# A two-layer encoder on one core: the row scale spread through memory, one multiply on VectorE, the last stores on one queue

## The chip, the core and the metric

The kernel runs on one core of a Trainium2 chip. Its engines work side by side, each through its own instructions in order, and wait for each other through semaphores: TensorE (PE in the profile; its weight loads are PEld), VectorE (DVE), ScalarE (ACT), GpSimd (POOL) and SyncE (SP), which here only issues DMAs. DMAs can be issued from SP, ACT or POOL; the transfers run on 16 DMA engines that all queues share. Matmul results land in PSUM, everything else on the chip lies in SBUF with 128 partitions, and "memory" means the DRAM beside the chip.

The metric is device time in microseconds of one execution. The kernel before was run three times.

## What is computed

A sequence of 256 tokens with 2048 features passes through two residual layers and a last RMS norm:

```
def rms_norm(x, g):
    xf = x.astype(jnp.float32)
    y = xf * lax.rsqrt(jnp.mean(xf * xf, axis=-1, keepdims=True) + EPS)
    return (y * g.astype(jnp.float32)).astype(x.dtype)

def reference(x, norm_g, final_g, w_in_even, w_out_even, rpb_b, w_in_odd, w_out_odd,
              sinks_c, qnorm_d, knorm_d):
    h = x
    for layer in range(DEPTH):
        y = rms_norm(h, norm_g[layer])
        i = layer // 2
        if layer % 2 == 0:
            h = h + even_layer(y, w_in_even[i], w_out_even[i], rpb_b[i])
        else:
            h = h + odd_layer(y, w_in_odd[i], w_out_odd[i], sinks_c[i], qnorm_d[i], knorm_d[i])
    return rms_norm(h, final_g)
```

Each layer multiplies the normed tokens by one wide input projection, runs two kinds of attention of 8 heads each on the results, gates them with a SiLU path, and multiplies by an output projection. All of it is float32.

## The kernel before

Every product is made from three matmuls: each float32 operand is split into a rounded high part and the remainder (`hi` and `lo`), and `mm3` (L100) adds hi·hi, hi·lo and lo·hi. Weights come from memory in blocks of 128 x 1024 (`Weights`, L54): SP loads the block into `wraw` (5 buffers), ScalarE writes `whi` (L69), VectorE writes `wlo` (L70), 3 buffers each. So each weight block costs one ScalarE and one VectorE instruction, and TensorE follows with the matmuls of that block. `by_feature` (L258) uses a block as the stationary operand (L267, L271), `by_token` (L277) as the moving one (L102 to L104).

The norm's gain per feature is multiplied into the tokens when they are split (`split`, L89, with `gcol`): ScalarE writes `xh` (L95) and VectorE `xl` (L96). The norm's scale per token, `r` or `rstd` (two columns of 128 tokens, L179), is not ready then; it is multiplied into the projections' results afterwards. Where tokens lie on partitions, a column of `r` does. Where tokens lie along the free axis (results of `by_feature`), every partition needs all 256 scales in a row. `spread_scale` (L187) makes that row: for each half a 128 x 128 tile `rb` whose row p holds the scale of token p (VectorE, from `ones`), a transpose of it on TensorE (L193) into the PSUM tile `ps_bc`, and a copy to `rk` (L196). From `rk` come `rq` (L197) and `rhalf` (L199), used in `scaled` (L307) for the queries, keys and gates. It runs once per layer: in `first_scale` (L585, near 43 us) and `second_scale` (L669, near 485 us).

The opening: 15 matmuls on zeros (`WARM`, L124) keep TensorE busy until the first operands arrive. The first product runs `by_token` over 8 blocks; with each block come two 128 x 256 blocks of x (`xraw`), split on the way (L71 to L74), and behind them the same x in the other layout (`load_h`, L136), whose squares give the first `r`.

The end: the last output product is made for token half 0, then for half 1 in two column halves. For each, `added` (L777) adds it to the residual and sums squares, `scale_of` (L788) makes the scale, and `finish` (L798) multiplies the four column blocks of 512 and stores each. Blocks 1 and 2 of half 1 are multiplied on ScalarE and stored from ACT's queue, the others are multiplied on VectorE and stored from SP's; blocks 0 and 3 are done in halves of 256 columns.

The order of instructions on each engine is fixed before the run by a planner that keeps the priority of program order but lets an instruction pass another that, by the planner's estimate of times, is not ready yet. What is wrapped in `pin`, `pinned` or `tc.keep_in_program_order` keeps its written order on its engine: nearly all DMAs on SP and the whole end.

Of the kernel before, what the change touches and what calls it, by code (L numbers as in the profile page):

```python
# [9 lines left out]
F32 = mybir.dt.float32  # L10
# [8 lines left out]
P = 128  # L19
D = 2048  # L20
S = 256
# [6 lines left out]
SCALE = HD ** -0.5  # L28
BIG = 1e30
GRID_W = 64  # L30
WARM = 15
AHEAD = 2
RPB_R, RPB_C = 15, 31

# [2 lines left out]
def encoder(ctx, tc, a, out):  # L37
    nc = tc.nc
    pool = lambda name, bufs, **kw: ctx.enter_context(tc.tile_pool(name=name, bufs=bufs, **kw))
    const = pool("const", 1)  # L40
# [4 lines left out]
    tp = pool("tp", 2)  # L45
    sm = pool("sm", 4)
    PS = bass.MemoryType.PSUM
    dram = pool("dram", 1, space=bass.MemoryType.DRAM)
    ps_mm = pool("ps_mm", 2, space=PS)
    ps_at = pool("ps_at", 3, space=PS)  # L50
# [3 lines left out]
    class Weights:  # L54


        def __init__(self, src, hi=None, lo=None, x=None):
            raw = wp.tile([P, 1024], F32, tag="wraw", name="wraw")
            self.hi = hi or hp.tile([P, 1024], F32R, tag="whi", name="whi")
            self.lo = lo or hp.tile([P, 1024], F32R, tag="wlo", name="wlo")  # L60
            cuts = KK if x in (0, 1) else 1
            cols = [slice(i * 1024 // cuts, (i + 1) * 1024 // cuts) for i in range(cuts)]
            for i, c in enumerate(cols):
                load = nc.sync.dma_start if x is None else pinned
                load(raw[:, c], src[:, c])
                if x is not None and i == 0:
                    pinned(xraw[x], a["xt"][x].rearrange("p (k t) -> p k t", k=KK))
            for i, c in enumerate(cols):
                nc.scalar.copy(self.hi[:, c], raw[:, c])  # L69
                nc.vector.tensor_sub(self.lo[:, c], raw[:, c], self.hi[:, c].bitcast(F32))  # L70
                if x is not None:  # L71
                    for m in (i,) if cuts > 1 else range(KK):
                        k = x * KK + m
                        split(xh[k], xl[k], xraw[x][:, m, :], gcol[:, k : k + 1])  # L74

    plan, ready = [], []

# [7 lines left out]
    def pinned(dst, src, **kw):  # L85

        tc.keep_in_program_order(nc.sync.dma_start(dst, src, **kw))

    def split(hi, lo, src, scale=None):  # L89

        if scale is None:
            nc.scalar.copy(hi, src)
            nc.vector.tensor_sub(lo, src, hi.bitcast(F32))
        else:
            nc.scalar.mul(hi, src, scale)  # L95
            nc.vector.scalar_tensor_tensor(  # L96
                out=lo, in0=src, scalar=scale, in1=hi.bitcast(F32), op0=ALU.mult, op1=ALU.subtract
            )
# [10 lines left out]
    xh = [X[k // 4][:, k % 4, 0, :] for k in range(KC)]  # L109
    xl = [X[k // 4][:, k % 4, 1, :] for k in range(KC)]  # L110
# [3 lines left out]
    xraw = [big.tile([P, KK, S], F32, tag=f"mh{j}", name="xraw") for j in range(NJ)]  # L114

    gcol = const.tile([P, 2 * KC], F32, tag="gcol", name="gcol")
# [6 lines left out]
    ps_idle = ps_o.tile([P, S], F32, tag="o", name="ps_idle")  # L123
    for _ in range(WARM):  # L124
        nc.tensor.matmul(ps_idle, idle[:, :P], idle, start=True, stop=True, skip_group_check=True)

    ident = const.tile([P, P], F32, tag="ident", name="ident")
    ones = const.tile([P, P], F32, tag="ones", name="ones")
    cosT = const.tile([P, 2, P], F32, tag="cosT", name="cosT")
    sinT = const.tile([P, 2, P], F32, tag="sinT", name="sinT")  # L130
    maskB = const.tile([P, S], F32, tag="maskB", name="maskB")
# [4 lines left out]
    def load_h(n):  # L136
        x = a["x"].rearrange("(t p) d -> p t d", p=P)
        pinned(h[n], x[:, :, n * 512 : (n + 1) * 512])
# [32 lines left out]
    def square_sums(parts, n, t=None):  # L171

        for tt in range(2) if t is None else (t,):
            junk = tp.tile([P, 512], BF16, tag="junk", name="junk", bufs=1)
            tc.keep_in_program_order(
                nc.scalar.activation(junk, h[n][:, tt, :], AF.Square, accum_out=parts[:, tt, n : n + 1])
            )
# [8 lines left out]

    def spread_scale(r):  # L187

        bc = ps_at.tile([P, S], F32, tag="at", name="ps_bc")
        for tt in range(2):  # L190
            t = tp.tile([P, P], F32, tag="rb", name="rb")
            nc.vector.tensor_scalar_mul(t, ones, r[:, tt : tt + 1])
            nc.tensor.transpose(bc[:, tt * P : (tt + 1) * P], t, ident)  # L193
        rk = const.tile([P, S], F32, tag="rk", name="rk")
        rq = const.tile([P, S], F32, tag="rq", name="rq")
        nc.vector.tensor_copy(rk, bc)  # L196
        nc.vector.tensor_scalar_mul(rq, rk, -SCALE)  # L197
        rhalf = const.tile([P, S], F32, tag="rhalf", name="rhalf")
        nc.vector.tensor_scalar_mul(rhalf, rk, 0.5)  # L199
        return rk, rq, rhalf  # L200
# [114 lines left out]
    def scaled_split(tag, acc, rbc):  # L315
        dst = pair(tag)
        split(*dst, scaled(acc, rbc))
        return dst

    def values(dst, acc, r):  # L320
        hi, lo = dst
        for t in range(2):
            split(hi[:, t, :], lo[:, t, :], acc[t], r[:, t : t + 1])
# [252 lines left out]
    def opening(j):  # L576
        if j == 2:
            make_identity(nc, ident)
            nc.gpsimd.memset(ones, 1.0)
        if j > 3:  # L580
            load_h(j - 4)
        if j == 7:
            square_sums(parts0, 0)

    def first_scale():  # L585
        for n in range(1, NN):
            square_sums(parts0, n)
            yield
        r = row_scale(0, parts0)
        yield  # L590
        yield
        scales[0] = r, spread_scale(r)
        yield
# [21 lines left out]
    for u in range(4):  # L615
        st = {}
        if u == 1:
            bg.append(later_consts())
        for pr, kind in even_order(u):
            if kind != "v":  # L620
                evac.append(evict_even(2 * u + pr, kind, by_feature(), st))
                continue
            if u:
                acc = by_token(512, token_acc())
            else:
                acc = [ps_at.tile([P, 512], F32, tag="at", name="ps_t") for _ in range(2)]
                by_token(512, acc, opening)
                evac.append(first_scale())
            st["v"] = values_tile()
            evac.append(evict_even(2 * u, kind, acc, st))  # L630
# [38 lines left out]
    def second_scale():  # L669
        for _ in range(4):  # L670
            yield
        scales[1] = spread_scale(r1)
        yield
# [88 lines left out]
    pin = tc.keep_in_program_order  # L762
    full, halves = slice(0, 512), [slice(0, 256), slice(256, 512)]
# [13 lines left out]
    def added(t, c, acc, others=None):  # L777
        ss = col("ss")
        add_y3(t, c, acc)
        junk = tp.tile([P, 512], BF16, tag="junk", name="junk", bufs=1)  # L780
        if others is None:
            pin(nc.scalar.activation(junk[:, c], y3(t, c), AF.Square, accum_out=ss))
        else:
            y = y3(t, c)
            pin(nc.vector.tensor_tensor_reduce(junk[:, c], y, y, 1.0, others, ALU.mult, ALU.add, ss))
        return ss

    def scale_of(ss, t):  # L788

        root, y, half, u, r = [col(name) for name in ("root", "y", "half", "u", "r")]  # L790
        pin(nc.scalar.activation(root, ss, AF.Sqrt, bias=sums[:, t : t + 1], scale=1.0 / D))
        pin(nc.vector.tensor_scalar(half, ss, -0.5 / D, minus[:, t : t + 1], ALU.mult, ALU.add))
        pin(nc.vector.reciprocal(y, root))
        pin(nc.vector.tensor_scalar(u, y, y, half, ALU.mult, ALU.mult))
        pin(nc.vector.tensor_scalar(r, u, 1.5, y, ALU.add, ALU.mult))
        return r

    def finish(n, t, r, cols=full, scalar=False):  # L798
        y = h[n][:, t, cols]
        if n == NN - 1:  # L800
            pin(nc.vector.scalar_tensor_tensor(y, y, r, gfin[n][:, cols], ALU.mult, ALU.mult))
        elif scalar:
            pin(nc.scalar.mul(y, y, r))  # L803
        else:
            pin(nc.vector.tensor_scalar_mul(y, y, r))
        queue = nc.scalar if scalar and t else nc.sync
        pin(queue.dma_start(out[t * P : (t + 1) * P, n * 512 + cols.start : n * 512 + cols.stop], y))

    for j, pr in enumerate(late):
        product_out(accs[0], final[j], pr, 0, False, j == 3)  # L810
    r = scale_of(added(0, full, accs[0]), 0)
    finish(0, 0, r)
    finish(2, 0, r, scalar=True)
    finish(1, 0, r)
    finish(3, 0, r)
    for j, pr in enumerate(late[:3]):
# [6 lines left out]
        ss = added(1, c, z[:, c], ss)  # L823
    r = scale_of(ss, 1)
    finish(0, 1, r, halves[0])
    finish(1, 1, r, scalar=True)
    finish(0, 1, r, halves[1])
    finish(2, 1, r, scalar=True)
    finish(3, 1, r, halves[0])
    finish(3, 1, r, halves[1])  # L830

# [82 lines left out]
```

## Time and profile before

| | us |
|---|---|
| three runs: median | 821.35 |
| lowest, highest | 820.9, 821.37 |
| profiled execution: time | 820.54 |
| its span, first to last instruction | 818.8 |
| TensorE clock granted, mean | 0.996 |

The span is the time that the profile shows; the 1.74 us between it and the execution's time lie outside the first and last instruction. Rows of the profile name an instruction by its line, engine and operation, then `out<-in`. In a timeline row the first number is the start in us from the span's start and the second the busy time; `x2` joins neighbours of one kind; the brackets give the engine's idle time before it and what ended that. ACTq, SPq and POOLq are the engines' own sequencers, which issue DMAs. A row `A <- B: 0.4, 1, 0.4` says that A waited for B for 0.4 us in total, once, at most 0.4.

### The profile page before, as it was taken

The numbers are of one execution on the slowest core, as the hardware profiler recorded it, in microseconds if no ns is written. First come the engines' busy times: TensorE is split into PE (matmuls) and PEld (weight loads), VectorE is DVE, ScalarE is ACT, GpSimd is POOL, SyncE is SP. The second block draws the span as 40 slices with busy tenths as digits, with TensorE's granted clock in tenths as the row PEclk, the third lists the DMA queues.
The fourth block names the chain that finished last, engine by engine and source line by source line (L and its number), as shares of the span: only waits on it lengthen the run. The fifth ranks groups of instructions, "written<-read, shape, count | busy, mean of one in ns | idle before, by whom it ended". The sixth has DMA issues, their size and how long they took to land.

```text
span 818.8 us, 11775 instructions
## 1 busy us (share of the span) xinstructions
PE 808.6 (99%) x4317; PEld 695.1 (85%) x4317; DVE 576.1 (70%) x856; ACT 447.3 (55%) x712; POOL 110.6 (14%) x88
## 2 busy tenths in 40 slices
PE   9999999999999999999999999999999999999995
PEld 7888888888888888888888888888899888888884
DVE  6677675677857886587655577685987777775763
ACT  7745454554545554455445544657666665664651
POOL 0002020021302140050200000002112222221000
PEclk9999999999999999999999999999999999999998
DMA  8956765575755766565654555556577775777532
GB/s 336 354 210 209 271 213 177 208 213 168 233 182 171 241 173 220 203 194 197 213 177 172 186 186 172 200 192 198 161 183 226 224 222 184 227 197 225 209 126 104
DMA packets 90682, 166.91 MB, mean 204 GB/s; under 512 B 48960, under 2 KB 50112, under 8 KB 90560
## 3 DMA queue, kind: packets, MB, share of 16 engines
q1 hardware_dynamic: 90192, 165.61, 62.5%
q8 instruction: 34, 0.56, 0.3%
q10 hardware_dynamic: 432, 0.54, 0.2%
q14 instruction: 24, 0.20, 0.1%
HBM read 155.64 MB, written 3.05 MB: 194 GB/s over the span
## 4 chain that ended last, share of the span: by engine, by line
PE 98%; DMA 0%; ACT 0%; DVE 0%; issue 0%; ACTq 0%; DVEq 0%
PE ps_f L267 34%; PE ps_f L271 17%; PE ps_t L102 14%; PE ps_t L103 14%; PE ps_t L104 14%; PE ps_s L103 1%; PE ps_s L104 1%; PE ps_s L102 1%; PE ps_out L103 1%; PE ps_out L102 1%; PE ps_out L104 1%; PE ps_ht L660 0%; DMA wraw<-in_even_t 0%; PE ps_tr L372 0%; ACT h L803 0%; ACT whi L69 0%
## 5 line engine op out<-in xcount | busy, mean ns | idle before, releaser
L70 DVE TENSOR_TENSOR wlo<-wraw,whi 128x1024 fp32r<-128x1024 f32 (+1 forms) x270 | 344.4, 1276 | 187.8 <-ACT whi L69 187.3
L69 ACT CAST whi<-wraw 128x1024 fp32r<-128x1024 f32 (+1 forms) x270 | 281.9, 1044 | 300.9 <-PE ps_t L104 130.7
L267 PE MATMUL ps_f<-x,whi 128*128 128x512 f32 x1184 | 372.3, 396 | 0.0
L271 PEld LDWEIGHTS ps_f<-x,wlo 128*128 128x128 f32 x1184 | 222.4, 188 | 52.9 <-DVE wlo L70 0.7
L271 PE MATMUL ps_f<-x,wlo 128*128 128x256 f32 x1184 | 233.0, 278 | 0.0
L267 PEld LDWEIGHTS ps_f<-x,whi 128*128 128x128 f32 x1184 | 180.9, 189 | 0.5
L102 PE MATMUL ps_t<-whi,x 128*128 128x512 f32 (+1 forms) x256 | 96.8, 381 | 0.3 <-ACT x L95 0.3
L103 PE MATMUL ps_t<-wlo,x 128*128 128x512 f32 (+1 forms) x256 | 96.4, 379 | 0.0
L104 PE MATMUL ps_t<-whi,x 128*128 128x512 f32 (+1 forms) x256 | 96.1, 377 | 0.0
L463 POOL COPY ph<-pr 128x1024 uint16<-128x1024 uint16 x32 | 39.5, 1233 | 418.1 <-ACT pr L453 252.0
L102 PE MATMUL ps_t<-whi,mh 128*128 128x512 f32 x240 | 93.8, 391 | 0.0
L103 PE MATMUL ps_t<-wlo,mh 128*128 128x512 f32 x240 | 93.7, 391 | 0.0
L104 PE MATMUL ps_t<-whi,ml 128*128 128x512 f32 x240 | 93.6, 390 | 0.0
L104 PEld LDWEIGHTS ps_t<-whi,x 128*128 128x128 f32 x256 | 48.5, 189 | 9.0
L102 PEld LDWEIGHTS ps_t<-whi,x 128*128 128x128 f32 x256 | 48.5, 189 | 9.0 <-ACT x L95 0.6
L474 POOL COPY pt<-pa 128x1024 uint16<-128x1024 uint16 x32 | 50.4, 1576 | 37.5 <-DMA pa<-ph 37.2
L103 PEld LDWEIGHTS ps_t<-wlo,x 128*128 128x128 f32 x256 | 48.6, 190 | 8.2
L104 PEld LDWEIGHTS ps_t<-whi,ml 128*128 128x128 f32 x240 | 45.1, 188 | 9.3
L103 PEld LDWEIGHTS ps_t<-wlo,mh 128*128 128x128 f32 x240 | 45.1, 188 | 8.9
L102 PEld LDWEIGHTS ps_t<-whi,mh 128*128 128x128 f32 x240 | 45.1, 188 | 8.9
L445 ACT ACTIVATE pr<-lg,mn 128x256 f32<-128x256 f32 (+1 forms) x48 | 24.0, 501 | 16.5 <-POOL ph L463 8.9
L403 POOL TENSOR_TENSOR bias<-maskB,rpb 128x512 f32<-128x512 f32 x8 | 12.5, 1567 | 138.5 <-DMA rpb<-rows 138.5
(129 smaller groups left out, 664.4 us busy)
## 6 DMA issues: line engine op xcount, KB each, us to landing
wraw<-in_even_f SPq DMA_DIRECT2D x96, 512.0 KB, 3.5
wraw<-in_odd_f SPq DMA_DIRECT2D x56, 512.0 KB, 3.7
wraw<-in_w_out_even SPq DMA_DIRECT2D x32, 512.0 KB, 3.3
wraw<-in_w_out_odd SPq DMA_DIRECT2D x32, 512.0 KB, 4.3
wraw<-in_even_t SPq DMA_DIRECT2D x30, 512.0 KB, 4.3
wraw<-in_odd_t SPq DMA_DIRECT2D x24, 512.0 KB, 3.2
xraw<-in_xt SPq DMA_DIRECT2D x8, 256.0 KB, 7.0
h<-in_x SPq DMA_DIRECT2D x4, 512.0 KB, 8.6
```

The source lines that it names most:

```text
L69: nc.scalar.copy(self.hi[:, c], raw[:, c])
L70: nc.vector.tensor_sub(self.lo[:, c], raw[:, c], self.hi[:, c].bitcast(F32))
L102: nc.tensor.matmul(dst, lh, rh, start=first, stop=False, skip_group_check=True)
L103: nc.tensor.matmul(dst, lh, rl, start=False, stop=False, skip_group_check=True)
L104: nc.tensor.matmul(dst, ll, rh, start=False, stop=last, skip_group_check=True)
L267: nc.tensor.matmul(acc[:, f, :], w.hi[:, c], xx[k], start=k == 0, stop=False, skip_group_check=True)
L271: nc.tensor.matmul(acc[:, f, :S], w.lo[:, c], xh[k], start=False, stop=k == KC - 1, skip_group_check=True)
L403: nc.gpsimd.tensor_tensor(b, maskB.unsqueeze(1).to_broadcast([P, 2, S]), raw, op=ALU.subtract)
L445: nc.scalar.activation(p[:, t, :W], lg[:, t, :W], AF.Exp, bias=mn[:, t : t + 1], scale=-1.0, accum_out=den[:, t : t + 1],)
L463: nc.gpsimd.tensor_copy(halves, words)
L474: nc.gpsimd.tensor_copy(words.bitcast(U16).rearrange("p c (q s) -> p s c q", s=2), st[i])
```

## The change

Three places. `spread_scale` no longer uses VectorE's `ones`, TensorE and PSUM: GpSimd's queue writes `r` to a line of 256 floats in memory, and then reads that line into all 128 partitions as `rk`. In the opening, the first block of x (k = 0) is multiplied on VectorE instead of ScalarE, and there are 14 matmuls on zeros instead of 15. At the end all five stores of token half 1 go through SP's queue, the two halves of block 0 follow each other, and block 3 is done whole.

```
-WARM = 15
+WARM = 14
...
-                        split(xh[k], xl[k], xraw[x][:, m, :], gcol[:, k : k + 1])
+                        split(xh[k], xl[k], xraw[x][:, m, :], gcol[:, k : k + 1], on=nc.vector if k == 0 else None)
...
-            nc.scalar.mul(hi, src, scale)
+            if on is None:
+                nc.scalar.mul(hi, src, scale)
+            else:
+                on.tensor_scalar_mul(hi, src, scale)
...
     def spread_scale(r):
 
-        bc = ps_at.tile([P, S], F32, tag="at", name="ps_bc")
-        for tt in range(2):
-            t = tp.tile([P, P], F32, tag="rb", name="rb")
-            nc.vector.tensor_scalar_mul(t, ones, r[:, tt : tt + 1])
-            nc.tensor.transpose(bc[:, tt * P : (tt + 1) * P], t, ident)
+        line = dram.tile([2, P], F32, tag="line", name="line")
+        nc.gpsimd.dma_start(line.rearrange("t p -> p t"), r)
         rk = const.tile([P, S], F32, tag="rk", name="rk")
+        nc.gpsimd.dma_start(rk, line.rearrange("t p -> (t p)").partition_broadcast(P))
         rq = const.tile([P, S], F32, tag="rq", name="rq")
-        nc.vector.tensor_copy(rk, bc)
         nc.vector.tensor_scalar_mul(rq, rk, -SCALE)
...
-        queue = nc.scalar if scalar and t else nc.sync
-        pin(queue.dma_start(out[t * P : (t + 1) * P, n * 512 + cols.start : n * 512 + cols.stop], y))
+        pin(nc.sync.dma_start(out[t * P : (t + 1) * P, n * 512 + cols.start : n * 512 + cols.stop], y))
...
     finish(0, 1, r, halves[0])
+    finish(0, 1, r, halves[1])
     finish(1, 1, r, scalar=True)
-    finish(0, 1, r, halves[1])
     finish(2, 1, r, scalar=True)
-    finish(3, 1, r, halves[0])
-    finish(3, 1, r, halves[1])
+    finish(3, 1, r)
```

The tile `ones` and its memset (L579) go as well.

More of the change, by code (lines that the diff above doesn't have):

```diff
@@ L87, in pinned, with split @@
         tc.keep_in_program_order(nc.sync.dma_start(dst, src, **kw))
-    def split(hi, lo, src, scale=None):
+    def split(hi, lo, src, scale=None, on=None):
         if scale is None:
@@ L127, in encoder @@
     ident = const.tile([P, P], F32, tag="ident", name="ident")
-    ones = const.tile([P, P], F32, tag="ones", name="ones")
     cosT = const.tile([P, 2, P], F32, tag="cosT", name="cosT")
@@ L578, in opening @@
             make_identity(nc, ident)
-            nc.gpsimd.memset(ones, 1.0)
         if j > 3:
```

## The prediction

> **What bounds the kernel now.** I read the page's busy times and its chain by engine first, then the busy time by stage (columns: stretch and length, then busy us and instructions of PE, PEld, DVE, ACT and POOL, the granted clock, DMA share, GB/s), then the waits of the first 30 us.
>
> ```profile
> PE 808.6 (99%) x4317; PEld 695.1 (85%) x4317; DVE 576.1 (70%) x856; ACT 447.3 (55%) x712; POOL 110.6 (14%) x88
> ...
> PE 98%; DMA 0%; ACT 0%; DVE 0%; issue 0%; ACTq 0%; DVEq 0%
> ```
>
> ```profile
> 60.00:480.00 420.00, 420.00 (x2272) 361.56 (x2271) 292.01 (x382) 215.32 (x311) 60.67 (x41) 1.00 0.62 202
> ...
> 500.00:800.00 300.00, 300.00 (x1617) 258.73 (x1616) 224.03 (x363) 179.22 (x318) 49.13 (x40) 1.00 0.63 195
> ```
>
> ```profile
> PEld ps_f L271 <- DVE wlo L70: 0.4, 1, 0.4
> ```
>
> TensorE is the path: 420.00 of 420.00 us and 300.00 of 300.00 us are busy at clock 1.00. In such a stretch a matmul less is time less, and work of another engine counts only when it makes TensorE wait. The last row is the exception: at 28.6 us TensorE once waits for a weight block. So the change is weighed in four places: the opening, the two spreads of the row scale (45 and 489 us), and the tail.
>
> **TensorE slots that go.** Four transposes (L193), two per layer.
>
> ```profile
> 42.92 0.63 PE L267 MATMUL ps_f<-x,whi 128*128 128x512 f32 x2
> ...
> 44.31 0.63 PE L267 MATMUL ps_f<-x,whi 128*128 128x512 f32 x2
> ...
> 45.02 0.38 PE L193 MATMUL ps_bc<-ident,rb 128*128 128x128 f32 x2
> ...
> 45.95 0.62 PE L267 MATMUL ps_f<-x,whi 128*128 128x512 f32 x2
> ```
>
> ```profile
> 488.50 0.39 PE L104 MATMUL ps_t<-whi,x 128*128 128x512 f32 x1
> ...
> 489.18 0.39 PE L104 MATMUL ps_t<-whi,x 128*128 128x512 f32 x1
> 489.41 0.38 PE L193 MATMUL ps_bc<-ident,rb 128*128 128x128 f32 x2
> ...
> 490.10 0.40 PE L104 MATMUL ps_t<-whi,x 128*128 128x512 f32 x1
> ```
>
> Durations overlap, so I take the distance of starts. In layer 0 two periods of the loop take 44.31 - 42.92 = 1.39 us, and 45.95 - 44.31 = 1.64 us with the transposes inside: 0.25 us. In layer 1 three matmuls take 489.18 - 488.50 = 0.68 us, and 490.10 - 489.18 = 0.92 us with them: 0.24 us. Nothing else fills these slots, so **-0.49 us**.
>
> **The scale through memory.** Two multiplies by `ones` and the copy out of PSUM leave VectorE. In their place POOL's queue, otherwise empty there, gets a store of 256 single floats and, behind its completion, a read of 1 KB into each of 128 partitions. No matmul reads `rk`; but VectorE runs in order, and `rq`, `rhalf` and the first product with `rq` stand among the weight blocks `wlo` that TensorE needs.
>
> ```profile
> 42.89 0.16 DVE L168 SCALAR_TENSOR_TENSOR rstd<-rs_t,rs_z 128x2 f32<-128x2 f32 x1
> ...
> 46.34 1.22 DVE L70 TENSOR_TENSOR wlo<-wraw,whi 128x1024 fp32r<-128x1024 f32 x1
> 47.47 0.29 DVE L197 TENSOR_SCALAR rq<-rk 128x256 f32<-128x256 f32 x1
> ...
> 47.88 0.69 DVE L312 TENSOR_TENSOR qf<-qf,rq 128x512 f32<-128x512 f32 x1
> 49.13 1.23 DVE L70 TENSOR_TENSOR wlo<-wraw,whi 128x1024 fp32r<-128x1024 f32 x1 [0.57 <-ACT whi L69]
> ...
> 490.70 1.22 DVE L70 TENSOR_TENSOR wlo<-wraw,whi 128x1024 fp32r<-128x1024 f32 x1
> ```
>
> ```profile
> 51.29 0.39 PE L271 MATMUL ps_f<-x,wlo 128*128 128x256 f32 x2
> ...
> 54.08 0.39 PE L271 MATMUL ps_f<-x,wlo 128*128 128x256 f32 x2
> ...
> 495.34 0.39 PE L103 MATMUL ps_t<-wlo,x 128*128 128x512 f32 x1
> ```
>
> ```profile
> rpb<-rows SPq DMA_DIRECT2D x32, 64.0 KB, 2.7
> ...
> sink<-in_sinks_c SPq DMA_DIRECT2D x1, 4.0 KB, 6.7
> ```
>
> ```profile
> DMA to landing us min/median/max: 1.9/2.6/3.3
> ```
>
> Counting weight blocks from the opening (2.79 us of TensorE each in layer 0, with three buffers of `wlo` running ahead), the `wlo` of 46.34 is first read at 51.29, that of 49.13 at 54.08, that of 490.70 at 495.34. The scale is ready at 43.05. If `rq` stays where it is, ahead of the block of 49.13, that block must start by 54.08 - 1.23 = 52.85, with 1.1 us (47.47 to 48.57) ahead of it: `rk` may land as late as 51.75, **8.7 us** after the scale. Should the order put `rq` one block earlier, the bound is 51.29 - 1.22 - 1.1 = 48.97, or **5.9 us**. Layer 1 has as much room: its block starts at 490.70 and is read 4.64 us later, against 4.95 us in both rows of layer 0.
>
> The trip itself is not in the trace. Stores land in 1.9 to 3.3 us (last row, those of `out`), reads in 2.7 (`rpb`, from the chip's memory) to 6.7 us (`sink`, in a burst). What POOL's queue takes to issue is not shown: between 0.33 us, an issue on SP (tail, below), and 1.04 us, the excess of a disturbed VectorE block over 1.23 us (below). I take 1.0 for each, since software on POOL is nearer to a POOL instruction: 2.0 + 2.6 + 2.7 = **7.3 us**, between 0.66 + 1.9 + 2.7 = 5.3 and 2.1 + 3.3 + 6.7 = 12.1. At 7.3 and the present order the cover holds: **0**, with 2 x 3.4 us at the far end. The attention that a later `rk` would delay starts only here:
>
> ```profile
> 65.68 0.42 DVE L429 CUSTOM_DVE_ANT_0 lg<-ps_s,bias 128x256 f32<-128x256 f32 x1
> ```
>
>
> The Trainium skill, page "DMA: Bandwidth & Descriptors", section "Anatomy of one DMA — SWDGE (gpsimd) path", fits about 2.0 us plus bytes over 436 GB/s per transfer; as an estimate that makes 2.0 + 2.3 = 4.3 us here, and the sum the same.
>
> **The opening.** One warm-up matmul goes, and the first multiply of `x` moves from ScalarE to VectorE.
>
> ```profile
> 4.50 0.69 DVE L70 TENSOR_TENSOR wlo<-wraw,whi 128x512 fp32r<-128x512 f32 x1 [3.35 <-ACT whi L69]
> 4.53 0.91 ACT L95 ACTIVATE x<-xraw,gcol 128x256 fp32r<-128x256 f32 x2
> 5.09 0.80 PE L102 MATMUL ps_t<-whi,x 128*128 128x512 f32 x1 [0.32 <-ACT x L95]
> ```
>
> ```profile
> 26.28 1.05 ACT L69 CAST whi<-wraw 128x1024 fp32r<-128x1024 f32 x1 [2.23 <-DMA wraw<-in_even_f]
> ```
>
> ```profile
> 27.36 1.23 DVE L70 TENSOR_TENSOR wlo<-wraw,whi 128x1024 fp32r<-128x1024 f32 x1 [2.08 <-ACT whi L69]
> ```
>
> ```profile
> 28.05 0.61 PE L267 MATMUL ps_f<-x,whi 128*128 128x512 f32 x2
> 28.64 0.50 PE L271 MATMUL ps_f<-x,wlo 128*128 128x256 f32 x2
> ```
>
> ```profile
> 2.00:26.00 24.00, 23.68 (x100) 19.68 (x100) 16.28 (x26) 15.88 (x28) 0.00 (x0) 1.00 1.00 377
> ```
>
> The nearest VectorE multiply of this size is 0.29 us (47.47), ScalarE's 0.91 / 2 = 0.45: the first matmul can start 0.2 us earlier, if the multiply goes ahead of `wlo`; behind it, 4.50 + 0.69 + 0.29 = 5.48, it starts 0.4 us later. Neither reaches the end in full. From 2 to 26 us the DMA engines are full (share 1.00, 377 GB/s); ScalarE gets the ninth block at 26.28 after 2.23 us of waiting for it, VectorE ends `wlo` at 28.59, and TensorE reads it at 28.64, some 0.12 us after it would have (28.05 + 0.47). A head start ends in that wait; a late one costs what exceeds 0.12. **0**, between -0.2 and +0.3. The warm-up matmul only frees an engine that then waits for `x`.
>
> **The tail.** Five stores on SP's queue instead of four there and two on ACT's, and ScalarE no longer issues between its two multiplies.
>
> ```profile
> 812.73 0.33 SPq L807 DMA_DIRECT2D out<-h  x1
> ```
>
> ```profile
> L807 SPq DMA_DIRECT2D out<-h x8: 332/382/448, 807.8 to 814.4; - x8
> ```
>
> ```profile
> 813.60:816.60 3.00, 0.00 (x0) 0.00 (x0) 0.15 (x1) 0.64 (x1) 0.00 (x0) 0.50 0.98 345
> ```
>
> The first half still leaves at 812.73, and from 813.6 to 816.6 the DMA engines are full (0.98): 1.05 MB at 345 GB/s is 3.0 us. Five issues 0.45 us apart reach 814.5, as late as now (814.4), with data always queued. Fewer small rows may help a little: **-0.1**, between -0.3 and +0.6 (a landing of 3.3 instead of 2.6 us).
>
> **Sum**: -0.49 + 0 + 0 - 0.1 = -0.6. The profiled execution would go from 820.54 to 819.9 (span 818.8 to 818.2). The median of the three runs, 821.35, stands 0.81 above that execution; from it the forecast is **820.8**.
>
> **Rivals.** *Slower: VectorE stands behind a late `rk`.* The point is 5.9 or 8.7 us for the trip. With 7.3 us and `rq` one block earlier TensorE loses 1.4 us per layer: 820.8 + 2.8 = **823.6**. For it speaks that the order is fixed before the run; against it, the present order and 2 us of margin at the short trip.
>
> *POOL and VectorE keep each other waiting.*
>
> ```profile
> 619.46 2.27 DVE L70 TENSOR_TENSOR wlo<-wraw,whi 128x1024 fp32r<-128x1024 f32 x1 [0.68 <-ACT whi L69]
> ```
>
> Here a `wlo` took 2.27 instead of 1.23 us while POOL copied. One such hold, 1.04 us, on each transfer makes the trip 9.4, 0.7 us over the bound per layer: 820.8 + 1.4 = **822.2**; with `rq` earlier as well, 3.5 per layer: 827.8. The Trainium skill, page "SBUF — State Buffer", section "SBUF: two separate sides", warns of it: transfers issued from GpSimd starve while VectorE runs a two-port operation, 3100 instead of 620 ns in its example. The trace agrees that the two engines hold each other; no run here yet shows it for a transfer.
>
> *The opening's head start survives*, because the loads come earlier than the trace suggests: 820.8 - 0.2 = **820.6**. *The parts don't do what they say*: the multiply sits behind `wlo` or the single queue ends late, +0.3 or +0.7, about **821.4**.
>
> **How the numbers follow.** A measurement of this kernel can tell about 0.2%, 1.6 us, from no change. Forecast 820.8 (820.2 to 821.3): 0.56. Head start: 0.06. Parts that don't act: 0.17. Late `rk`: 0.14. Mutual waiting: 0.07. The last two pass +1.6 us for most of their weight, 0.14. No case here passes -1.6 us; for what the trace does not show I leave 0.03. Within: 0.83. The range runs from all gains together, 820.8 - 0.2 - 0.2 - 0.4 of spread between runs = 820.0, to 823.0, inside the late `rk`.
>
> **What would show it.** Right: no L193; loop starts near 45 and 489 us at even distance; TensorE without a wait between 30 and 800; the wait for `wlo` near 28.6 still there, longer by the head start; stores full from 813 to 816. Wrong: a wait of TensorE for `wlo` just after 50 or 492 us, VectorE idle before L197 for over 4 us, or a stretch after the last store that is longer than now.

## The result, and the profile after

| | before | after |
|---|---|---|
| median, us | 820.97 (6 runs) | 838.81 (6 runs) |
| lowest to highest, us | 820.64 to 821.37 | 836.98 to 840.17 |
| ratio after / before | | 1.0215 (1.0201 to 1.0228) |
| profiled execution: time, us | 820.54 | 839.16 |
| its span, us | 818.8 | 837.3 |

The changed kernel is slower by 17.84 us. The forecast was 820.8 us, with a range up to 823.0. The line numbers below are those of each kernel's own file. In the changed kernel the store of the scale is L192, its read back L194, `rq` L196, `rhalf` L198, and `spread_scale`'s transposes are gone; `ps_f` is made at L266 and L270, `mm3` is L105 to L107.

First the page after: the busy times, then the chain that ended last, by engine and by line.

```profile
PE 814.2 (97%) x4312; PEld 698.3 (83%) x4312; DVE 573.2 (68%) x850; ACT 447.0 (53%) x711; POOL 114.2 (14%) x91
...
PE 93%; DMA 4%; DVE 1%; ACT 0%; issue 0%; ACTq 0%; DVEq 0%; POOLq 0%
PE ps_f L266 32%; PE ps_f L270 16%; PE ps_t L106 13%; PE ps_t L105 13%; PE ps_t L107 13%; DMA line<-rstd 2%; DMA rk<-line 1%; PE ps_s L107 1%; PE ps_s L106 1%; PE ps_s L105 1%; PE ps_out L106 1%; PE ps_out L105 1%; PE ps_out L107 1%; DVE wlo L70 1%; PE ps_ht L658 0%; DMA wraw<-in_even_t 0%
```

TensorE has 5 matmuls fewer and is busy 5.6 us longer (814.2 against 808.6), so it also ran slower somewhere; and the chain, 98% TensorE before, now holds 3% of the two new transfers. Where that happened shows in the busy time by stage of the changed kernel (columns as in the prediction).

```profile
36.00:60.00 24.00, 19.71 (x113) 16.83 (x111) 10.38 (x23) 10.08 (x17) 1.44 (x2) 0.97 0.87 175
60.00:480.00 420.00, 418.38 (x2260) 360.58 (x2261) 293.15 (x383) 216.04 (x308) 59.72 (x41) 0.99 0.62 201
500.00:800.00 300.00, 294.22 (x1576) 252.84 (x1575) 218.00 (x356) 175.11 (x312) 51.55 (x41) 0.99 0.65 199
```

TensorE is idle for 4.29 us between 36 and 60 us, for 1.62 us just behind, and for 5.78 us once between 500 and 800 us. The waits of the changed kernel name the cause (total, times, longest):

```profile
DVE rq L196 <- DMA rk<-line: 20.4, 2, 10.3
...
POOL rk L194 <- DMA line<-rstd: 17.1, 2, 8.7
...
PE ps_f L270 <- DVE wlo L70: 5.9, 1, 5.9
PE ps_t L106 <- DVE wlo L70: 5.8, 1, 5.8
```

TensorE waits twice for a weight block, VectorE stands twice for some 10 us in front of `rq`, and GpSimd twice for over 8 us for its own store. This is the chain, read from the bottom up. VectorE's timeline in layer 0 (start, busy, instruction, idle time before it):

```profile
44.59 0.16 DVE L170 SCALAR_TENSOR_TENSOR rstd<-rs_t,rs_z 128x2 f32<-128x2 f32 x1
...
46.13 1.40 DVE L99 SCALAR_TENSOR_TENSOR vl<-ps_t,rstd,vh 128x512 fp32r<-128x512 f32 x2
47.82 1.23 DVE L70 TENSOR_TENSOR wlo<-wraw,whi 128x1024 fp32r<-128x1024 f32 x1 [0.29 <-ACT whi L69]
59.34 0.29 DVE L196 TENSOR_SCALAR rq<-rk 128x256 f32<-128x256 f32 x1 [10.29 <-DMA rk<-line]
...
60.35 1.22 DVE L70 TENSOR_TENSOR wlo<-wraw,whi 128x1024 fp32r<-128x1024 f32 x1
```

The scale is ready at 44.59 + 0.16 = 44.75 us; `rq` starts at 59.34. The order is that of the kernel before, one `wlo` between `vl` and `rq`; the next `wlo` stands behind `rq` and starts 10 us late. GpSimd's timeline, both layers, and the landing times (KB each, us from issue to landing) between 45 and 55 us:

```profile
45.07 0.86 POOL L192 DMA_DIRECT2D line<-rstd  x1 [43.77 <-DVE rstd L170]
54.38 0.58 POOL L194 DMA_DIRECT2D rk<-line  x1 [8.45 <-DMA line<-rstd]
...
494.61 0.79 POOL L192 DMA_DIRECT2D line<-rstd  x1 [86.60 <-DVE rstd L170]
504.09 0.57 POOL L194 DMA_DIRECT2D rk<-line  x1 [8.69 <-DMA line<-rstd]
```

```profile
wraw<-in_even_f SPq DMA_DIRECT2D x2, 512.0 KB, 10.6
rk<-line POOLq DMA_DIRECT2D x1, 128.0 KB, 4.9
line<-rstd POOLq DMA_DIRECT2D x1, 1.0 KB, 9.0
```

The store of 1 KB lands 9.0 us after its issue, the read of 128 KB takes 4.9 us. Two weight loads issued beside the store land in 10.6 us, three times what they take elsewhere (3.3 us between 42 and 55 us before). What TensorE does then, and the clock granted to it in stretches of 2 us:

```profile
55.08 0.63 PE L266 MATMUL ps_f<-x,whi 128*128 128x512 f32 x2
61.62 0.79 PE L270 MATMUL ps_f<-x,wlo 128*128 128x256 f32 x2 [5.91 <-DVE wlo L70]
62.22 1.05 PE L266 MATMUL ps_f<-x,whi 128*128 128x512 f32 x2
```

```profile
58.00:60.00 2.00, 0.00 (x0) 0.00 (x0) 0.66 (x3) 0.00 (x0) 0.00 (x0) 0.64 0.23 47
60.00:62.00 2.00, 0.38 (x1) 0.38 (x2) 2.00 (x3) 1.53 (x3) 0.00 (x0) 0.50 0.00 0
...
64.00:66.00 2.00, 2.00 (x10) 1.72 (x8) 2.00 (x3) 0.85 (x2) 0.00 (x0) 0.66 0.71 231
```

A pair of matmuls takes 1.05 us instead of 0.63 after the wait: while TensorE stood still its clock was halved. A mean of 0.64 over 58 to 60 us puts the fall at 58.6 us, 2.9 us after TensorE ran dry (55.7), and 0.66 over 64 to 66 puts the return at 65.4: 6.8 us at half clock, of which TensorE worked 3.7 and lost half, 1.9 us. In layer 1 the clock is at half from 509.1 to 515.9 us, 6.8 us too, but the fall comes 4.6 us after TensorE ran dry. The Trainium skill, page "TensorE: Matmul & The Clock Gate", section "What's actually happening", says that the clock falls to half after an idle window of about 3.4 us and comes back after a busy one. The 6.8 us fit two such windows; but the fall in layer 0, 2.9 us after TensorE ran dry, came before a full one had passed.

ScalarE's `whi` casts serve as marks for the accounts, since each stands for a certain weight block. Two blocks, before and after:

```profile
48.05 1.05 ACT L69 CAST whi<-wraw 128x1024 fp32r<-128x1024 f32 x1 [1.97 <-PE ps_f L267]
...
61.94 1.05 ACT L69 CAST whi<-wraw 128x1024 fp32r<-128x1024 f32 x1 [1.69 <-PE ps_f L267]
```

```profile
49.52 1.05 ACT L69 CAST whi<-wraw 128x1024 fp32r<-128x1024 f32 x1 [1.74 <-PE ps_f L266]
...
71.31 1.05 ACT L69 CAST whi<-wraw 128x1024 fp32r<-128x1024 f32 x1 [1.69 <-PE ps_f L266]
```

The first mark is late by 1.47 us, the second by 9.37: layer 0 lost 7.90 us, the wait of 5.91 and 2.0 at half clock. In layer 1 the same marks go from 495.31 to 504.36 (+9.05) and from 500.75 to 518.48 (+17.73): 8.68 us, the wait of 5.77 and 2.9 at half clock. The remaining terms of the span's 18.5 us are the 1.47 up to the first mark (1.70 in the opening of this execution, less 0.23 for layer 0's two transposes), -0.3 from 71 to 504 us, where layer 1's two transposes went, 0.5 near 616 us, where weight loads of TensorE waited for VectorE twice (0.21 and 0.45 us), and 0.3 behind the last scale (6.97 us to the end instead of 6.70).

### The profile page after: what moved, and what is told of

Read it like the earlier page. It is cut to its first block, busy times and chain, and to the rows that moved or that the text cites. A ratio compares the mean times of both kernels' runs of the same rounds, so it can differ in the third digit from the quotient of the medians.

```text
span 837.3 us, 11761 instructions
## 1 busy us (share of the span) xinstructions
PE 814.2 (97%) x4312; PEld 698.3 (83%) x4312; DVE 573.2 (68%) x850; ACT 447.0 (53%) x711; POOL 114.2 (14%) x91
## 4 chain that ended last, share of the span: by engine, by line
PE 93%; DMA 4%; DVE 1%; ACT 0%; issue 0%; ACTq 0%; DVEq 0%; POOLq 0%
PE ps_f L266 32%; PE ps_f L270 16%; PE ps_t L106 13%; PE ps_t L105 13%; PE ps_t L107 13%; DMA line<-rstd 2%; DMA rk<-line 1%; PE ps_s L107 1%; PE ps_s L106 1%; PE ps_s L105 1%; PE ps_out L106 1%; PE ps_out L105 1%; PE ps_out L107 1%; DVE wlo L70 1%; PE ps_ht L658 0%; DMA wraw<-in_even_t 0%
## 5 line engine op out<-in xcount | busy, mean ns | idle before, releaser
L266 PE MATMUL ps_f<-x,whi 128*128 128x512 f32 x1184 | 373.2, 397 | 0.0
L270 PEld LDWEIGHTS ps_f<-x,wlo 128*128 128x128 f32 x1184 | 223.0, 189 | 59.6 <-DVE wlo L70 7.1
L270 PE MATMUL ps_f<-x,wlo 128*128 128x256 f32 x1184 | 233.7, 279 | 5.9 <-DVE wlo L70 5.9
L266 PEld LDWEIGHTS ps_f<-x,whi 128*128 128x128 f32 x1184 | 181.5, 189 | 0.5
L106 PE MATMUL ps_t<-wlo,x 128*128 128x512 f32 (+1 forms) x256 | 98.2, 386 | 5.8 <-DVE wlo L70 5.8
L105 PE MATMUL ps_t<-whi,x 128*128 128x512 f32 (+1 forms) x256 | 98.2, 385 | 1.3 <-DVE x L98 1.3
L107 PE MATMUL ps_t<-whi,x 128*128 128x512 f32 (+1 forms) x256 | 97.3, 383 | 0.0
L105 PE MATMUL ps_t<-whi,mh 128*128 128x512 f32 x240 | 93.8, 391 | 0.0
L107 PE MATMUL ps_t<-whi,ml 128*128 128x512 f32 x240 | 93.5, 390 | 0.0
L105 PEld LDWEIGHTS ps_t<-whi,x 128*128 128x128 f32 x256 | 49.4, 193 | 10.4 <-ACT x L96 1.5
L107 PEld LDWEIGHTS ps_t<-whi,x 128*128 128x128 f32 x256 | 49.5, 193 | 9.3
L107 PEld LDWEIGHTS ps_t<-whi,ml 128*128 128x128 f32 x240 | 45.1, 188 | 9.3
L105 PEld LDWEIGHTS ps_t<-whi,mh 128*128 128x128 f32 x240 | 45.1, 188 | 9.0
```

The source lines that it names most:

```text
L105: nc.tensor.matmul(dst, lh, rh, start=first, stop=False, skip_group_check=True)
L106: nc.tensor.matmul(dst, lh, rl, start=False, stop=False, skip_group_check=True)
L107: nc.tensor.matmul(dst, ll, rh, start=False, stop=last, skip_group_check=True)
L266: nc.tensor.matmul(acc[:, f, :], w.hi[:, c], xx[k], start=k == 0, stop=False, skip_group_check=True)
L270: nc.tensor.matmul(acc[:, f, :S], w.lo[:, c], xh[k], start=False, stop=k == KC - 1, skip_group_check=True)
```

## The experiments

The theory after the result: the whole loss is the scale's way through memory, and in it the store, 256 separate pieces of 4 bytes that land next to each other in memory. Rivals: GpSimd's software queue is what is slow; VectorE's port keeps GpSimd from issuing; the read is; the opening and the tail carry a good part. Times are medians, the kernel before was timed along with each run, and every comparison of several runs has its 95% interval.

**The three parts, each alone.** `spread_only` is the kernel before with `spread_scale` as changed, `start_only` with 14 warm-up matmuls and the first block of x on VectorE, `tail_only` with the changed last stores.

> The kernel before with the scale spread through memory alone. Theory (VectorE stands behind a late rk, and TensorE runs out of weight blocks): the two waits of 5.9 and 5.8 us for wlo return, each followed by some 5 us of TensorE at half pace (2 to 2.7 us lost each), less 0.49 us for the transposes: about +15.8 us, 836.8. Rival (the loss of the changed kernel lies as much in the opening and the end, and the spread costs only its two waits): +11 us, 832.

> The kernel before with 14 warm-up matmuls and the first multiply of x on VectorE. Theory (the multiply stands behind wlo, TensorE idles over 1 us after the warm-up and stays at half pace until about 10.7 us instead of 7.3): the first product starts 0.5 to 0.7 us later and the first block of the next product 1.8 us later, +1.8 us, 822.8. Rival (the loads bind the opening, as the prediction had it): TensorE still waits for the block near 28.6 us and the time is the same within 0.3 us.

> The kernel before with the new order of the last stores on one queue. Theory of the prediction (the DMA engines are full to the end, the queue does not matter): -0.1 us, between -0.3 and +0.3. Rival (in the changed kernel the DMA share drops to 0.39 for half a microsecond between the second and the third store; a single queue starves the engines): +0.4 to +0.8 us.

| | us | lowest to highest | before | ratio |
|---|---|---|---|---|
| `spread_only` | 836.99 (4 runs) | 835.75 to 840.04 | 820.99 | 1.0201 (1.0184 to 1.0219) |
| `start_only` | 821.46 (10 runs) | 821.09 to 822.54 | 820.99 | 1.0007 (0.9998 to 1.0017) |
| `tail_only` | 821.62 (11 runs) | 820.96 to 822.27 | 820.99 | 1.0008 (0.9999 to 1.0016) |

The differences, 16.0, 0.5 and 0.6 us, sum to 17.1 of the 17.84; the rest is within the spread of the four runs of `spread_only`. Its waits and landing times show the changed kernel's picture again, with one store still later, so that the median of two is 10.8 us:

```profile
PE ps_t L103 <- DVE wlo L70: 7.9, 1, 7.9
PE ps_f L267 <- DVE wlo L70: 5.9, 1, 5.9
```

```profile
line<-rstd POOLq DMA_DIRECT2D x2, 1.0 KB, 10.8
```

`start_only` missed its expectation. The multiply does stand behind `wlo`, which starts at 4.83 us: the multiply starts at 5.44, and the first product at 5.93 instead of 5.09 us. But the 1.5 us that the changed kernel's profile lost by 48 us isn't the price of that. Half of it is a stretch in which the first matmuls run at half pace, and how long that lasts differs between executions: to 7.0 us in the profile of before, to 8.6 in that of `start_only`, to 10.7 in that of the changed kernel, and to 10.6 in that of `spread_only`, whose opening is unchanged. The Trainium skill, page "TensorE: Matmul & The Clock Gate", section "What's actually happening", calls the length of this stretch variable from run to run; the rows agree. `warm_fill` tests the rest: 18 warm-up matmuls instead of 14, so that TensorE is idle for a shorter time before the first product.

```
-WARM = 15
+WARM = 18
```

(with the multiply on VectorE as in `start_only`)

> The kernel before with the first multiply of x on VectorE and 18 warm-up matmuls instead of 14. Theory (the idle time after the warm-up keeps TensorE at half pace for one stretch more): without the gap the pace doubles near 7.3 us again, the first product starts as late as with 14, and of the 1.8 us some 1.5 come back: +0.3 us. Rival (only the late multiply counts): as start_only, +1.8 us.

It took 821.03 us (10 runs, 820.4 to 822.01) against 821.01, ratio 1.0001 (0.9992 to 1.001). The idle time before the first product fell from 1.38 to 0.65 us and the product ran at full pace at once; yet the time is that of before, 0.4 us below `start_only`, a difference that these runs don't tell from none. The opening is not where the loss is.

In `tail_only` the five stores are not issued at even distance: 814.04, 814.48, then 815.25 us. ScalarE's two multiplies for the third and fourth store ran from 813.66 for 1.33 us, so the third one's data were ready at about 814.4; why SP issues it 0.9 us later is not shown. The DMA engines' share in stretches of half a microsecond shows what it costs:

```profile
814.50:815.00 0.50, 0.00 (x0) 0.00 (x0) 0.44 (x1) 0.49 (x1) 0.00 (x0) 0.50 0.20 70
...
816.50:817.00 0.50, 0.00 (x0) 0.00 (x0) 0.00 (x0) 0.00 (x0) 0.00 (x0) 0.50 1.01 381
```

The engines are full only from 816.5 us, not from the first store on; before, with the stores on two queues, their share was 0.81 in the half microsecond in which data began to move and 1.00 in the next. From the last scale to the span's end it takes 6.89 us instead of 6.70, so the trace accounts for 0.2 of the 0.6 us, which isn't clear of zero itself.

**Is it GpSimd's queue?** `store_act` issues the store from ScalarE's hardware queue and leaves the read on GpSimd's. Its edit and the next ones are shown against `spread_only`.

```
-        nc.gpsimd.dma_start(line.rearrange("t p -> p t"), r)
+        nc.scalar.dma_start(line.rearrange("t p -> p t"), r)
```

> The spread through memory alone, with the store of the 256 scales issued from ACT's queue and the read left on POOL's. Theory (the form of the store, 256 pieces of 4 bytes, makes it late): it lands 7 to 9 us after its issue as before, TensorE waits twice for 5 to 6 us, +15 us. Rival (POOL's software queue is the slow part): it lands in 2 to 3.3 us like the stores of out, the trip falls from 14.3 to about 8 us, and TensorE's waits vanish: within 1 us of the kernel before.

One run took 835.98 us against 821.01. The landing time is 7.9 us and TensorE still waits:

```profile
line<-rstd ACTq DMA_DIRECT2D x2, 1.0 KB, 7.9
```

```profile
PE ps_f L267 <- DVE wlo L70: 4.9, 2, 4.4
PE ps_t L103 <- DVE wlo L70: 4.5, 1, 4.5
```

So the queue is some 1 us of the store's 9, and not its cause.

**Is it the form of the store?** `store_rows` turns `r` by one transpose on TensorE into two partitions of 128 scales, and stores these as two rows of 512 bytes; the read stays.

```
+        nc.tensor.transpose(bc[:2, :], r, ident)
...
+        nc.vector.tensor_copy(row[:2, :], bc[:2, :])
...
-        nc.gpsimd.dma_start(line.rearrange("t p -> p t"), r)
+        nc.gpsimd.dma_start(line, row[:2, :])
```

> The spread through memory with the scales first turned into two rows of 128 on TensorE (one transpose, one copy out of PSUM), so that POOL's store has two pieces of 512 bytes instead of 256 of 4 bytes; queues unchanged. Theory (the form of the store): it lands in 2 to 4 us, the weight loads beside it keep their 3 to 4 us, the trip is 8 to 9 us, and TensorE waits at most 1 us per layer: +0 to +3 us. Rival (POOL's queue): 7 to 9 us to landing as before, +15 us.

```profile
rk<-line POOLq DMA_DIRECT2D x2, 128.0 KB, 4.3
...
line<-row POOLq DMA_DIRECT2D x2, 1.0 KB, 2.2
```

The same 1 KB from the same queue lands in 2.2 us. After the opening no matmul waits for `wlo` any more; VectorE waits 5.3 us before `rq` in two goes without holding anybody up, and the time is 821.59 us (10 runs, 820.82 to 822.71) against 821.01, ratio 1.0005 (0.9996 to 1.0015). The read, which is the same, is not what made the trip late. But the store's form is not all that differs, as VectorE's rows in layer 0 show:

```profile
47.51 1.23 DVE L70 TENSOR_TENSOR wlo<-wraw,whi 128x1024 fp32r<-128x1024 f32 x1
50.41 1.23 DVE L70 TENSOR_TENSOR wlo<-wraw,whi 128x1024 fp32r<-128x1024 f32 x1 [1.68 <-ACT whi L69]
...
53.91 0.29 DVE L197 TENSOR_SCALAR rq<-rk 128x256 f32<-128x256 f32 x1 [2.26 <-DMA rk<-line]
```

The order of instructions changed with the edit. Two weight blocks stand between `vl` and `rq` instead of one, and in layer 1 four stand between the scale and `rq` instead of two, so `rq` may come later. The scale is ready at 44.44 and 486.22 us, and `rq` starts 9.5 and 12.9 us later, in layer 1 because the transpose runs only at 490.62. In the order of the changed kernel, whose cover is 8.7 us in layer 0 and 8.6 in layer 1 (trip less wait), such trips would cost waits of 0.8 and 4.3 us, an estimate. So these runs show that rows land early and that a spread of this kind costs nothing clear of noise; what an earlier landing is worth in an unchanged order, `store_pairs` shows below. `after_rows` puts this store into the changed kernel:

> The changed kernel with the scales turned into two rows of 512 bytes on TensorE before the store (as in store_rows), all else as changed. Theory (the small store is all of the loss but about 1 us): no wait of TensorE near 60 or 505 us, and the time is that of the kernel before plus what opening, end and the rows showed alone, 0.5 + 0.6 + 0.6: 822.7, between 821 and 823.5. Rival (opening and end cost more beside the memory trip): over 825.

It took 822.61 us (10 runs, 821.59 to 823.73) against 821.1, ratio 1.0019 (1.0009 to 1.0028). The rows, with the later `rq` that came with them here too, take away 16 of the 17.84 us, and what is left, 1.5 us, fits the 1.7 of opening (0.5), tail (0.6) and `store_rows` itself (0.6).

**Is it VectorE's order?** `pool_scale` keeps the slow store, but makes `rq` and `rhalf` on GpSimd, so that VectorE doesn't stand in front of them.

```
-        nc.vector.tensor_scalar_mul(rq, rk, -SCALE)
+        nc.gpsimd.tensor_scalar_mul(rq, rk, -SCALE)
```

(and `rhalf` likewise)

> The spread through memory alone, with rq and rhalf computed on POOL instead of VectorE. Theory (what costs is that VectorE stands in order behind rk): in layer 1, where rk is first used some 40 us later, VectorE no longer waits and TensorE's second wait vanishes with its half-pace stretch, about 8 us; in layer 0 the first product with rq still stands in VectorE's order, so one wait of 6 us or more stays: +8 us, 829. Rival (the small store slows the weight loads, and these hold TensorE): both waits stay, +15 us or more.

It took 830.65 us (4 runs, 829.18 to 831.75) against 821.01, ratio 1.0114 (1.0096 to 1.0132). The store still landed late (8.9 us), but of the two waits only layer 0's is left; there the first product with `rq` is next in VectorE's order, and now stands where `rq` stood:

```profile
DVE qf L308 <- POOL rq L193: 10.8, 1, 10.8
...
PE ps_f L267 <- DVE wlo L70: 6.2, 1, 6.2
```

So a late scale costs only where an instruction that needs it stands ahead of a weight block that TensorE needs.

**What makes the store slow: pieces, their size, or their neighbours?** `store_pairs` stores both scales of a token as one piece of 8 bytes (128 pieces, the line in the order token, half, put right by a copy on VectorE). `store_double` stores every scale twice, 512 pieces of 4 bytes, and reads back the first 256.

```
+        line = dram.tile([P, 2], F32, tag="line", name="line")
+        nc.gpsimd.dma_start(line, r)
...
```

```
...
+        line = dram.tile([4, P], F32, tag="line", name="line")
+        nc.gpsimd.dma_start(line.rearrange("t p -> p t"), four)
...
```

> The spread through memory with the line laid out so that each partition's two scales lie side by side: POOL's store has 128 pieces of 8 bytes instead of 256 of 4; VectorE puts the row in order after the read. Theory (the landing grows with the number of small pieces): about 5 us to landing instead of 9, the trip about 10 us, TensorE waits 1 to 2 us per layer, 826 us. Rival (any store in pieces of a few bytes lands late, whatever their number): 9 us, 837.

> The spread through memory with the scales stored twice: 512 pieces of 4 bytes instead of 256, the read as before. Theory (landing grows with the number of pieces): 16 to 18 us to landing, the trip 22 us, each of TensorE's waits 8 us longer: 853 us. Rival (number does not matter): 9 us, 837.

```profile
line<-rstd POOLq DMA_DIRECT2D x2, 1.0 KB, 4.2
```

```profile
line<-four POOLq DMA_DIRECT2D x2, 2.0 KB, 10.8
```

The pairs land in 4.2 us, with VectorE's order as in the changed kernel. `rq` starts 9.9 and 10.3 us after the scale instead of 14.6 and 14.3, and TensorE's waits of 5.91 and 5.77 us shrink to these:

```profile
PE ps_t L103 <- DVE wlo L70: 1.8, 1, 1.8
PE ps_f L269 <- DVE wlo L70: 1.3, 1, 1.3
```

The clock doesn't fall, and the one run took 825.63 us against 821.1. So in the same order an earlier landing takes away most of the loss. The doubled store, expected to land late in proportion, lands no later than that of `spread_only`, 10.8 us (one run, 841.83 us). So the number of pieces doesn't set the time.

The last two take the spread as it was before and only add a store per layer that nobody reads. `alone_apart` puts each scale into its own 64 bytes in layer 0 and packs them as the change does in layer 1; `alone_column` packs one column, 128 pieces, in layer 0, and puts 256 apart in layer 1.

```
+        if layer == 0:
+            line = dram.tile([2, P, 16], F32, tag="apart", name="apart")
+            nc.gpsimd.dma_start(line.rearrange("t p w -> p t w")[:, :, 0], r)
+        else:
+            line = dram.tile([2, P], F32, tag="line", name="line")
+            nc.gpsimd.dma_start(line.rearrange("t p -> p t"), r)
...
```

> The kernel before, whose row scale still goes through TensorE, with an added store of the 256 scales from POOL that nobody reads: in layer 0 each scale into 64 bytes of its own, in layer 1 packed as in the change. Theory (a store lands late where several DMA engines write pieces of one short stretch of memory): 3 to 4 us in layer 0, 9 us or more in layer 1. Rival (256 pieces of 4 bytes are late wherever they lie): 9 us in both. As nobody waits for the store, the time should be that of the kernel before within 1 us by either, unless the weight loads it slows hold TensorE.

> As alone_apart, but in layer 0 only one column of 128 scales is stored, packed, and in layer 1 each of the 256 scales goes into 64 bytes of its own. Theory (sharing of a short stretch): layer 0 lands late, 6 to 9 us, layer 1 in 3 to 4 us. Rival (number of 4-byte pieces): about half of 9 us in layer 0, 9 us in layer 1. Third (only pieces of 4 bytes, in any number and place): 9 us in both. Time as the kernel before within 1 us.

The landing times of `alone_apart` between 42 and 55 us (layer 0) and, behind the dots, between 484 and 498 us (layer 1), then the same of `alone_column`:

```profile
wraw<-in_even_f SPq DMA_DIRECT2D x5, 512.0 KB, 3.3
apart<-rstd POOLq DMA_DIRECT2D x1, 1.0 KB, 3.5
...
wraw<-in_odd_t SPq DMA_DIRECT2D x5, 512.0 KB, 10.1
line<-rstd POOLq DMA_DIRECT2D x1, 1.0 KB, 9.0
```

```profile
wraw<-in_even_f SPq DMA_DIRECT2D x5, 512.0 KB, 8.2
column<-rstd POOLq DMA_DIRECT2D x1, 0.5 KB, 9.4
...
wraw<-in_odd_t SPq DMA_DIRECT2D x6, 512.0 KB, 3.5
apart<-rstd POOLq DMA_DIRECT2D x1, 1.0 KB, 3.5
```

In both layers 256 pieces of 4 bytes, each in its own 64 bytes, land in 3.5 us; 128 pieces packed side by side take 9.4, 256 packed 9.0. So neither pieces of 4 bytes as such nor their number make the store late: packing them side by side does. And the weight loads in flight go with it, 10.1 and 8.2 us beside a packed store, 3.3 and 3.5 beside a spread one. Neither kernel loses time, 821.27 us (10 runs, ratio 1.0002, 0.9993 to 1.0012) and 821.1 (10 runs, ratio 1.0000, 0.9991 to 1.0009) against 821.01: the buffers of weights cover a delay of 7 us where VectorE doesn't wait as well.

**What stays open.** Why packed pieces of 4 bytes are slow is not shown. That they wait for each other within a stretch of memory would fit, but then the pairs, packed too, have to be quick because a stretch holds half as many, or because 8 bytes suffice; no run tells these apart. Why one packed store in each of `spread_only` and `store_double` took over 12 us isn't known either. The changed kernel with its scales apart wasn't tried, since the read would then pick 256 pieces for each partition. No version tried beats the kernel before.

## Why the prediction was wrong, point by point

**What bounds the kernel: right.** Only what made TensorE wait counted. The places named, the opening, the two spreads and the tail, are where the time changed.

**Transposes, -0.49: right.** The four matmuls are gone and nothing fills their slots; the marks move by -0.23 us across them in layer 0 and by -0.26 in layer 1.

**Scale through memory, 0: the step that failed.** Its cover was right: 8.7 us with the present order, and the order stayed. With the measured trip, 59.34 - 44.75 = 14.6 us, the prediction's own bound gives a wait of 5.9 us; TensorE waited 5.91. The same bound gives the waits of layer 0 in the runs that keep the order: trips of 14.5 us (`spread_only`), 13.1 (`store_act`) and 9.9 (`store_pairs`) leave 5.8, 4.4 and 1.2, and 5.9, 4.4 and 1.3 were measured. The trip was mis-sized, and in it the store: 2.6 us taken, 3.3 at most, 9.0 measured. The error was to take the landing time of the stores of `out` for it. Those write rows, this one writes single words packed side by side, and the form counts: 2.2 us in rows, 3.5 as words apart, 9.0 packed. The read took 4.9 and 4.5 us, within its bounds (2.7 to 6.7) but well above the 2.7 taken; GpSimd's issue took 0.86 and 0.58 us, near the 1.0 taken. With the read alone at 4.9 the trip would have been 2.0 + 2.6 + 4.9 = 9.5 us and the wait 0.8: the store decided. So the upper bound, 12.1 us, was too low, and the price of passing it as well: the far end was put at 3.4 us per layer, and a wait of 5.9 cost 7.9, because the clock falls behind it. Even the prediction's own far end, 2 x 3.4 us over 820.8, lay outside the range it gave. Nothing in the trace of before shows a long wait of TensorE in mid-kernel, and the prediction had no term for what follows one.

The estimate from the Trainium skill, page "DMA: Bandwidth & Descriptors", section "Anatomy of one DMA — SWDGE (gpsimd) path", 4.3 us for both transfers, failed with it: about 14 us measured. For the store in rows the 2.2 us agree with its 2.0. The same page of the Trainium skill, in section "Specifications", asks for at least 512 bytes per transfer for full rate, below which the engine reads, modifies and writes. That rule speaks against this change and was not weighed. The runs bear it out in part: rows of 512 bytes are quick and packed words slow, but words apart, far below 512 bytes too, land in 3.5 us.

**Opening, 0 between -0.2 and +0.3: size.** The multiply went behind `wlo`, which the prediction named as the later case; alone it measures +0.5 us, with an interval from -0.2 to +1.4.

**Tail, -0.1 between -0.3 and +0.6: size.** Alone +0.6 us, with an interval from -0.1 to +1.3. "Five issues 0.45 us apart" with "data always queued" was wrong: the third issue came 0.77 us after the second, and the engines stood partly empty for 2 us.

**Rivals.** *VectorE behind a late `rk`* is what happened, by its mechanism and place, with a trip twice as long as its condition took, and at the later of its two points. Its price was 1.4 us per layer instead of 7.9 and 8.7. The "2 us of margin at the short trip" held against it don't come out of the prediction's figures, which leave 1.4 us at the trip taken (8.7 - 7.3) and 3.4 at the short one (8.7 - 5.3). *POOL and VectorE keep each other waiting* did not: GpSimd's issues took 0.57 to 0.86 us, and VectorE was idle for the second half of the store. No delay of the kind that the Trainium skill, page "SBUF — State Buffer", section "SBUF: two separate sides", warns of shows in these runs; the store was as late from ScalarE's queue, to within 1.1 us. The head start did not survive.

**What would show it.** "A wait of TensorE for `wlo` just after 50 or 492 us, VectorE idle before L197 for over 4 us" was the right sign to look for: both were there, at 55.7 and 504.5 us, VectorE idle for 10.3 and 10.1 us.

## What to carry to other kernels

A transfer's price is that of its form: before a DMA is priced by the landing time of another, compare the pieces it writes, their size and whether they lie side by side in memory, not the bytes; 1 KB cost 2.2 us here in two rows and 9.0 as 256 packed words. A wait for a DMA put on an engine that works in order costs everything queued behind it, so look for the first instruction behind it that the bounding engine needs, and count the buffers up to there. Where the bounding engine is TensorE, a wait of over 4 us cost another 1.5 to 3 us at half clock in these runs.

## What was not expected of the hardware

A packed store of 1 KB held up the other transfers. Weight loads of 512 KB in flight beside it landed in 8.2 to 10.6 us instead of 3.3 to 3.5, while the DMA engines moved next to nothing; from 48 to 50 us of the changed kernel their mean busy share is 1.00 and they move 8 GB/s:

```profile
48.00:50.00 2.00, 2.00 (x14) 1.74 (x13) 1.04 (x1) 0.48 (x1) 0.00 (x0) 1.00 1.00 8
```

A busy share alone would have read as a full memory path. In stretches this short it isn't a share of time either: the two microseconds before read 1.93, and beside the packed store of `alone_apart` two neighbouring stretches read 2.43 and 0.00.

The granted clock fell to half, for 6.8 us as a rule and 10.2 once in `store_double`, after each wait of TensorE of 4.4 us or more (`store_act`, `pool_scale`, `spread_only`, `store_double`, the changed kernel), 2.4 to 4.7 us after TensorE ran dry, and did not after waits of 1.3 and 1.8 us (`store_pairs`). The granted clock in the rows reads 1.00 in the opening while the first matmuls run at half pace, so there the durations tell more than the clock.
